# Delta-rule triangular doubling: small products of consecutive issue moved to different partition quarters, one PSUM bank per step

## The chip, the cores and the metric

The kernel runs on one core of a Trainium2 chip. The metric is the device time of one execution in microseconds, as the median over several runs. Lower is better.

## The reference, cut to what matters

The program is two residual blocks with many matrix products. The part at issue is the gated delta rule of the first block: per head it solves a unit lower triangular system for each chunk of the sequence.

```python
kk = jnp.einsum('cbhtd,cbhsd->cbhts', kc, kc)
a_mat = jnp.where(strict, bc[..., :, None] * kk * decay_mat, 0.0)
lhs = a_mat + jnp.eye(CHUNK, dtype=a_mat.dtype)
rhs = jnp.concatenate([vc * bc[..., None], kc * (bc * jnp.exp(gam))[..., None]], axis=-1)
sol = lax.linalg.triangular_solve(lhs, rhs, left_side=True, lower=True, unit_diagonal=True)
```

There are 16 heads of width 128 and 256 positions. Around it stand the large projections: x (256 x 2048) times weights of 2048 x about 20,000 columns in the first block, and more in the second.

## The kernel before, in words

The kernel keeps the large products exact enough by splitting each operand into a high and a low part (`hi`, `lo`) and issuing three matmuls for each weight tile: L156, L157 and L158 in the helper `proj_T` (256 columns, output tile `pT`) and L171, L172 and L173 in the helper `proj` (512 columns, output tile `pN`). ScalarE writes `hi` (L139) and VectorE `lo` (L140). These products fill TensorE through the whole program.

The delta rule is worked in four groups of four heads (`for hg in range(4)`), with the sequence in two halves of 128 positions, so that a group holds eight 128 x 128 triangular matrices, `i = 0..7`. `Ud(i // 4, i % 4)` is the strictly upper part of matrix `i`; `X` becomes the inverse of the unit triangular matrix. It is built by doubling: VectorE inverts the 16 x 16 diagonal blocks (`Xs`), and they come back through DRAM as `Xd` (128 partitions x 8 matrices x 32 columns, the partition quarter `Q[q]` holding the diagonal 32 x 32 block `q`), with the transposed blocks in `Gd`. Then:

- 16 to 32: for each quarter q and matrix i, `wp` = U block times G block (L651), ScalarE copies `-wp` to `W` (L652), `cp` = W times X (L656), and VectorE copies the new 16 x 16 corner to `Xd` (L658). VectorE transposes `Xd` to `Gd` (L659), GpSimd spreads them into `X` and `G` (L661, L663).
- 32 to 64: the same for the pairs of quarters (0, 1) and (2, 3): `wp` (L669), `W` (L670), `cp` (L674), copy to `X` (L675); and the transposed corner `gp_` (L678), copied to `G` (L679).
- 64 to 128: products of 64 x 64 (L683, L688); then the solution is applied with products of 128 x 128 (L695, L699, L703 and on).

Each small product reads its stationary and its moving operand from one quarter of the partitions and writes one quarter: in the first step, quarter q to quarter q; in the second, rows of quarter 0 to quarter 1, and 2 to 3, and back. A small product is one matmul in the program; in fp32 the trace shows two weight loads and two matmul records for it, called two passes here. `side()` hands out one of four buffers of one PSUM bank each (pool `psB`), in turn. In the kernel before, L651 and L656 have two buffers each, used by quarters of even and of odd number, and every quarter of the second step has a buffer of its own; so two quarters that follow one another lie in different banks. Where two runs of the loop share a buffer (`wps[0]` for quarters 0 and 2), the second waits until ScalarE has read the first.

The order on each engine is set by a scheduler when the program is built: it fills the waits of this chain with the projections' matmuls, which are independent of it. TensorE then takes its instructions in that order.

Of the kernel before, what the change touches and what calls it, by code (L numbers as in the profile page):

```python
# [11 lines left out]
AF = mybir.ActivationFunctionType  # L12
# [4 lines left out]
P = 128  # L17
# [67 lines left out]
def hybrid_block_kernel(  # L85
# [4 lines left out]
    act, ve, pe, gp = nc.scalar, nc.vector, nc.tensor, nc.gpsimd  # L90
# [13 lines left out]
    def side(shape=(P, 512), name="s"):  # L104
        return psB.tile(list(shape), F32, tag="s", name=name)
# [94 lines left out]
    with ExitStack() as b1:  # L200
# [139 lines left out]
        with s1:  # L340
# [46 lines left out]
            cps = side([P, 2, 24], name="cps")  # L387
# [131 lines left out]
        with ExitStack() as s2:  # L519
# [37 lines left out]
            XX = X.rearrange("p a b c -> p (a b) c")  # L557
            G = dn.tile([64, 8, 64], F32, name="G")
            gp.memset(X, 0.0)
            gp.memset(G[0:32, :, 32:64], 0.0)  # L560
            zt = dk.tile([P, 256], F32, tag="W", name="zt")
            gp.memset(zt, 0.0)
            nc.sync.dma_start(dram_x.rearrange("m s c -> (m s c)").rearrange("(p c) -> p c", p=P), zt)
            for hg in range(4):
# [46 lines left out]
                Ud = (lambda tt, h: U0[:, h, 0, 0:P] if tt == 0 else U1[:, h, 0, :])  # L611
# [17 lines left out]
                Xd = dn.tile([P, 8, 32], F32, tag="Xd", name="Xd")  # L629
                Gd = dn.tile([P, 8, 32], F32, tag="Gd", name="Gd")  # L630
# [14 lines left out]

                Q = [slice(32 * q, 32 * q + 32) for q in range(4)]
                W = dk.tile([P, 8, 32], F32, tag="W", name="W")
                wps = [side([P, 8, 32], name="wp") for _ in range(2)]
                for q in range(4):
                    for i in range(8):  # L650
                        pe.matmul(wps[q % 2][Q[q], i, :], Ud(i // 4, i % 4)[Q[q], Q[q]], Gd[Q[q], i, :], start=True, stop=True)  # L651
                    act.activation(W[Q[q]], wps[q % 2][Q[q]], AF.Copy, scale=-1.0)  # L652
                cps = [side([P, 8, 32], name="cp") for _ in range(2)]
                for q in range(4):
                    for i in range(8):
                        pe.matmul(cps[q % 2][Q[q], i, :], W[Q[q], i, :], Xd[Q[q], i, :], start=True, stop=True)  # L656
                    r = slice(32 * q, 32 * q + 16)
                    ve.tensor_copy(Xd[r, :, 16:32], cps[q % 2][r, :, 16:32])  # L658
                ve.transpose(Gd, Xd)  # L659
                for q in range(4):  # L660
                    gp.tensor_copy(XX[Q[q], :, Q[q]], Xd[Q[q]])  # L661
# [1 line left out]
                    gp.tensor_copy(G[Q[q], :, Q[q]], Gd[Q[q]])  # L663

                W = dk.tile([P, 8, 32], F32, tag="W", name="W")
                for q in (0, 2):
                    wp = side([P, 8, 32], name="wp")
                    for i in range(8):
                        pe.matmul(wp[Q[q + 1], i, :], Ud(i // 4, i % 4)[Q[q], Q[q + 1]], Gd[Q[q], i, :], start=True, stop=True)  # L669
                    act.activation(W[Q[q + 1]], wp[Q[q + 1]], AF.Copy, scale=-1.0)  # L670
                for q in (0, 2):
                    cp = side([P, 8, 32], name="cp")
                    for i in range(8):
                        pe.matmul(cp[Q[q], i, :], W[Q[q + 1], i, :], Xd[Q[q + 1], i, :], start=True, stop=True)  # L674
                    ve.tensor_copy(XX[Q[q], :, Q[q + 1]], cp[Q[q]])  # L675
                gp_ = side([P, 8, 32], name="gp_")
                for i in range(8):
                    pe.matmul(gp_[Q[1], i, :], Xd[Q[1], i, :], W[Q[1], i, :], start=True, stop=True)  # L678
                ve.tensor_copy(G[Q[1], :, Q[0]], gp_[Q[1]])  # L679

                wp = side([P, 8, 64], name="wp")
                for i in range(8):
                    pe.matmul(wp[64:P, i, :], Ud(i // 4, i % 4)[0:64, 64:P], G[:, i, :], start=True, stop=True)  # L683
                W = dk.tile([P, 8, 64], F32, tag="W", name="W")
                act.activation(W[64:P], wp[64:P], AF.Copy, scale=-1.0)
                cp = side([P, 8, 64], name="cp")
# [6 lines left out]
                wp = side([P, 4, P], name="wp")  # L693
# [3 lines left out]
                cp = side([P, 4, P], name="cp")  # L697
# [3 lines left out]
                wp = side([P, 4, P], name="wp")  # L701
# [162 lines left out]
        with ExitStack() as s4:  # L864
# [66 lines left out]
            for n in range(4):  # L931
# [3 lines left out]
                for kk in range(4):  # L935
                    ps = side([P, T], name="ps")
                    for t in range(2):
# [3 lines left out]
                                   scale=gx[:, 0, k:k + 1], bias=modT[:, 0, k:k + 1])  # L941
# [570 lines left out]
```

## Time and profile before

| | before |
|---|---|
| median of 3 runs (range) | 1936.2 us (1931.1 to 1937.52) |
| profiled execution: time, span | 1928.47 us, 1926.6 us |
| TensorE busy with matmuls | 1892.6 us (98%) |
| VectorE, ScalarE, GpSimd busy | 1491.6, 928.7, 256.7 us |
| granted TensorE clock, mean of the span | 0.995 |

The profiled execution's own time is 7.7 us below the median; what is added to or taken from its span is applied to the median. Busy time of TensorE counts matmuls that overlap one another in a pipeline; what one of them costs is read from the distance between starts.

### The profile page before, as it was taken

Reading aid. Unit: us, or ns where it says so; the run is one execution under the profiler, and the core shown is the slowest. Engines: PE = TensorE matmul, PEld = TensorE weight load, DVE = VectorE, ACT = ScalarE, POOL = GpSimd, SP = SyncE. Lnnn points to the kernel's source line nnn. Section 1 sums busy time; section 2 is a strip of 40 time slices with the busy share of each in tenths; the row PEclk is TensorE's granted clock in tenths of the full one; section 3 lists DMA queues with packets and bytes.
Section 4 is the critical chain, followed back from the end, with each engine's and each line's share of the span. In section 5 each row is a group of like instructions: output and inputs, shape, how many; then the busy total and the mean of one; then the engine's idle time right before and its main releaser. Section 6 shows DMA issues by size and latency. Waiting matters only on the chain. (4 is left out here: it accounts for less than half of the span.)

```text
span 1926.6 us, 31678 instructions
## 1 busy us (share of the span) xinstructions
PE 1892.6 (98%) x12358; PEld 1676.7 (87%) x12358; DVE 1491.6 (77%) x2141; ACT 928.7 (48%) x1240; POOL 256.7 (13%) x371
## 2 busy tenths in 40 slices
PE   9999999999999999999999999999999999999997
PEld 9989898999878898888888887889999998988776
DVE  6978687684648999879995558698787768878976
ACT  7645444453434443444444356663333355555553
POOL 1011010101101221112120000000000023301311
PEclk9999999999999999999999999999999999999999
DMA  8555454454545778768887576663343387557975
GB/s 294 168 165 169 153 169 155 143 176 137 164 158 198 240 258 264 242 222 266 283 284 245 194 258 227 199 212 116 126 148 120 122 288 204 166 174 256 300 248 178
DMA packets 123974, 389.76 MB, mean 202 GB/s; under 512 B 15408, under 2 KB 21976, under 8 KB 123312
## 3 DMA queue, kind: packets, MB, share of 16 engines
q1 hardware_dynamic: 95296, 314.44, 48.7%
q0 software_dynamic: 19296, 54.19, 9.7%
q10 hardware_dynamic: 9232, 19.11, 2.9%
q8 instruction: 97, 1.59, 0.3%
q14 instruction: 53, 0.43, 0.1%
HBM read 368.50 MB, written 16.03 MB: 200 GB/s over the span
## 5 line engine op out<-in xcount | busy, mean ns | idle before, releaser
L139 ACT ACTIVATE hi<-w 128x1024 fp32r<-128x1024 f32 (+1 forms) x535 | 559.1, 1047 | 711.3 <-PE pN L173 393.5
L140 DVE TENSOR_TENSOR lo<-w,hi 128x1024 fp32r<-128x1024 f32 (+1 forms) x535 | 647.7, 1213 | 266.1 <-ACT hi L139 256.7
L172 PE MATMUL pN<-lo,uh 128*128 128x512 f32 x768 | 306.2, 399 | 0.0
L171 PE MATMUL pN<-hi,uh 128*128 128x512 f32 x768 | 304.7, 397 | 0.0
L173 PE MATMUL pN<-hi,ul 128*128 128x512 f32 x768 | 304.5, 396 | 0.0
L156 PE MATMUL pT<-uh,hi 128*128 128x256 f32 x896 | 255.5, 285 | 2.2 <-ACT kq L754 1.9
L158 PE MATMUL pT<-uh,lo 128*128 128x256 f32 x896 | 256.5, 286 | 0.0
L157 PE MATMUL pT<-ul,hi 128*128 128x256 f32 x896 | 255.7, 285 | 0.0
L171 PEld LDWEIGHTS pN<-hi,uh 128*128 128x128 f32 x768 | 145.0, 189 | 33.8
L173 PEld LDWEIGHTS pN<-hi,ul 128*128 128x128 f32 x768 | 145.0, 189 | 33.2
L172 PEld LDWEIGHTS pN<-lo,uh 128*128 128x128 f32 x768 | 145.1, 189 | 33.1
L156 PEld LDWEIGHTS pT<-uh,hi 128*128 128x128 f32 x896 | 168.7, 188 | 5.2 <-ACT kq L754 2.1
L158 PEld LDWEIGHTS pT<-uh,lo 128*128 128x128 f32 x896 | 168.8, 188 | 2.9 <-issue 2.4
L473 DVE SCALAR_TENSOR_TENSOR ma<-m,sc,ma 128x512 f32<-128x512 f32 x240 | 171.1, 749 | 0.0
L157 PEld LDWEIGHTS pT<-ul,hi 128*128 128x128 f32 x896 | 168.8, 188 | 1.8 <-issue 1.2
L463 POOL DMA_DIRECT2D m<-in_w_mod_dram x128 | 69.5, 543 | 287.7 <-DVE ma L473 206.1
L139 ACT ACTIVATE hi<-TT 128x1024 fp32r<-128x1024 f32 x56 | 59.6, 1065 | 77.2 <-PE pK L1064 54.6
L140 DVE TENSOR_TENSOR lo<-TT,hi 128x1024 fp32r<-128x1024 f32 x56 | 68.4, 1223 | 21.0 <-ACT hi L139 20.6
L156 PE MATMUL pT<-hxh,hi 128*128 128x256 f32 x256 | 73.7, 288 | 1.8 <-ACT ra L1165 1.8
L157 PE MATMUL pT<-hxl,hi 128*128 128x256 f32 x256 | 73.0, 285 | 0.0
L158 PE MATMUL pT<-hxh,lo 128*128 128x256 f32 x256 | 73.0, 285 | 0.0
L172 PE MATMUL pN<-lo,hxh 128*128 128x512 f32 x160 | 63.7, 398 | 1.9 <-DVE lo L140 1.8
(729 smaller groups left out, 4053.1 us busy)
## 6 DMA issues: line engine op xcount, KB each, us to landing
w<-in_dn_qkv_dram SPq DMA_DIRECT2D x88, 512.0 KB, 3.2
m<-in_w_mod_dram POOLq DMA_DIRECT2D x128, 256.0 KB, 4.1
w<-in_dn_z_dram SPq DMA_DIRECT2D x32, 512.0 KB, 3.2
w<-in_ml_v_dram SPq DMA_DIRECT2D x32, 512.0 KB, 3.8
w<-in_ml_z_dram SPq DMA_DIRECT2D x32, 512.0 KB, 4.2
w<-in_ml_o_dram SPq DMA_DIRECT2D x32, 512.0 KB, 4.1
w<-in_gate_a_dram SPq DMA_DIRECT2D x32, 512.0 KB, 4.4
w<-in_gate_b_dram SPq DMA_DIRECT2D x32, 512.0 KB, 4.4
```

The source lines that it names most:

```text
L139: act.activation(hi, raw, AF.Copy)
L140: last_lo[0] = ve.tensor_tensor(lo, raw, hi.bitcast(F32), ALU.subtract)
L156: pe.matmul(o, hi[:, k, :], xh[:, kt, :], start=(kt == 0), stop=False)
L157: pe.matmul(o, hi[:, k, :], xl[:, kt, :], start=False, stop=False)
L158: pe.matmul(o, lo[:, k, :], xh[:, kt, :], start=False, stop=(kt == KT - 1))
L171: pe.matmul(ps[:, t, :], xh[:, kt, s], hi[:, k, :], start=(kt == 0), stop=False)
L172: pe.matmul(ps[:, t, :], xh[:, kt, s], lo[:, k, :], start=False, stop=False)
L173: pe.matmul(ps[:, t, :], xl[:, kt, s], hi[:, k, :], start=False, stop=(kt == KT - 1))
L463: (gp if g < 8 else nc.sync).dma_start(raw, d["w_mod"][g, kt])
L473: ve.scalar_tensor_tensor(a, raw, s, a, ALU.mult, ALU.add)
```

## The change

In each step the loops over quarter and matrix are turned: the matrix is now the outer loop and the quarter the inner one, so that consecutive products lie on different quarters. All quarters of a step write one buffer (one bank). In the first step one ScalarE instruction of 128 partitions replaces four of 32 partitions. In the second step the products of `cp` and `gp_` are issued in one loop. The arithmetic of each product stays as it is.

```diff
                 W = dk.tile([P, 8, 32], F32, tag="W", name="W")
-                wps = [side([P, 8, 32], name="wp") for _ in range(2)]
+                wp = side([P, 8, 32], name="wp")
+                for i in range(8):
+                    for q in range(4):
+                        pe.matmul(wp[Q[q], i, :], Ud(i // 4, i % 4)[Q[q], Q[q]], Gd[Q[q], i, :], start=True, stop=True)
+                act.activation(W, wp, AF.Copy, scale=-1.0)
+                cp = side([P, 8, 32], name="cp")
+                for i in range(8):
+                    for q in range(4):
+                        pe.matmul(cp[Q[q], i, :], W[Q[q], i, :], Xd[Q[q], i, :], start=True, stop=True)
                 for q in range(4):
-                    for i in range(8):
-                        pe.matmul(wps[q % 2][Q[q], i, :], Ud(i // 4, i % 4)[Q[q], Q[q]], Gd[Q[q], i, :], start=True, stop=True)
-                    act.activation(W[Q[q]], wps[q % 2][Q[q]], AF.Copy, scale=-1.0)
-                cps = [side([P, 8, 32], name="cp") for _ in range(2)]
-                for q in range(4):
-                    for i in range(8):
-                        pe.matmul(cps[q % 2][Q[q], i, :], W[Q[q], i, :], Xd[Q[q], i, :], start=True, stop=True)
                     r = slice(32 * q, 32 * q + 16)
-                    ve.tensor_copy(Xd[r, :, 16:32], cps[q % 2][r, :, 16:32])
+                    ve.tensor_copy(Xd[r, :, 16:32], cp[r, :, 16:32])
                 ve.transpose(Gd, Xd)
...
                 W = dk.tile([P, 8, 32], F32, tag="W", name="W")
+                wp = side([P, 8, 32], name="wp")
+                for i in range(8):
+                    for q in (0, 2):
+                        pe.matmul(wp[Q[q + 1], i, :], Ud(i // 4, i % 4)[Q[q], Q[q + 1]], Gd[Q[q], i, :], start=True, stop=True)
                 for q in (0, 2):
-                    wp = side([P, 8, 32], name="wp")
-                    for i in range(8):
-                        pe.matmul(wp[Q[q + 1], i, :], Ud(i // 4, i % 4)[Q[q], Q[q + 1]], Gd[Q[q], i, :], start=True, stop=True)
                     act.activation(W[Q[q + 1]], wp[Q[q + 1]], AF.Copy, scale=-1.0)
-                for q in (0, 2):
-                    cp = side([P, 8, 32], name="cp")
-                    for i in range(8):
-                        pe.matmul(cp[Q[q], i, :], W[Q[q + 1], i, :], Xd[Q[q + 1], i, :], start=True, stop=True)
-                    ve.tensor_copy(XX[Q[q], :, Q[q + 1]], cp[Q[q]])
+                cp = side([P, 8, 32], name="cp")
                 gp_ = side([P, 8, 32], name="gp_")
                 for i in range(8):
+                    for q in (0, 2):
+                        pe.matmul(cp[Q[q], i, :], W[Q[q + 1], i, :], Xd[Q[q + 1], i, :], start=True, stop=True)
                     pe.matmul(gp_[Q[1], i, :], Xd[Q[1], i, :], W[Q[1], i, :], start=True, stop=True)
+                for q in (0, 2):
+                    ve.tensor_copy(XX[Q[q], :, Q[q + 1]], cp[Q[q]])
                 ve.tensor_copy(G[Q[1], :, Q[0]], gp_[Q[1]])
```

Line numbers up to L656 are the same in both kernels; behind it the changed kernel's are two to five higher. The scheduler places the chain anew, so the order moves on every engine of this stage. Three places on TensorE follow; a name's number tells buffers apart, and `x8` means eight matmuls of that kind in a row.

TensorE, first head group, the second half of L651 and the first half of L656 in the kernel before (21 matmuls of `pT` stand between the first half of L651 and this):

```order
L157 MATMUL pT_2400<-ul_95,hi_2493 128x256
L651 MATMUL wp_1538<-Gd_1113,U0_1026 32x32 x4
L651 MATMUL wp_1538<-Gd_1113,U1_1027 32x32 x4
L651 MATMUL wp_1539<-Gd_1113,U0_1026 32x32 x4
L651 MATMUL wp_1539<-Gd_1113,U1_1027 32x32 x4
L656 MATMUL cp_1576<-Xd_1112,W_1537 32x32 x8
L656 MATMUL cp_1577<-Xd_1112,W_1537 32x32 x8
L158 MATMUL pT_2400<-uh_94,lo_2494 128x256
```

In the changed kernel, the same head group: all of L651 in one stretch.

```order
L157 MATMUL pT_2393<-ul_95,hi_2456 128x256
L651 MATMUL wp_1538<-Gd_1113,U0_1026 32x32 x16
L651 MATMUL wp_1538<-Gd_1113,U1_1027 32x32 x16
L158 MATMUL pT_2393<-uh_94,lo_2457 128x256
L156 MATMUL pT_2393<-uh_94,hi_2456 128x256
```

Three stretches (half of L651; the other half with half of L656; the rest of L656) have become two, L651 and, 24 matmuls of `pT` behind it, L656 with 32 matmuls into one `cp`.

TensorE, first head group, second step, the kernel before: `cp` of quarter 0, `cp` of quarter 2, then `gp_`.

```order
L158 MATMUL pT_2400<-uh_94,lo_2614 128x256
L674 MATMUL cp_1642<-Xd_1112,W_1621 32x32 x8
L674 MATMUL cp_1652<-Xd_1112,W_1621 32x32 x8
L678 MATMUL gp__1662<-W_1621,Xd_1112 32x32 x8
L156 MATMUL pT_2400<-uh_94,hi_2613 128x256
```

The changed kernel at this place (the pair of rows in the middle comes eight times in all):

```order
L157 MATMUL pT_2393<-ul_95,hi_2576 128x256
L677 MATMUL cp_1636<-Xd_1112,W_1616 32x32 x2
L678 MATMUL gp__1637<-W_1616,Xd_1112 32x32
L677 MATMUL cp_1636<-Xd_1112,W_1616 32x32 x2
L678 MATMUL gp__1637<-W_1616,Xd_1112 32x32
```

The two quarters of `cp` and the one of `gp_` now alternate; the number of products is the same, 24.

TensorE, last head group, the steps to 64 and 128, the kernel before:

```order
L173 MATMUL pN_6327<-hi_6468,ul_95 128x512
L674 MATMUL cp_5494<-Xd_4964,W_5473 32x32 x8
L674 MATMUL cp_5504<-Xd_4964,W_5473 32x32 x8
L678 MATMUL gp__5514<-W_5473,Xd_4964 32x32 x8
L683 MATMUL wp_5524<-G_950,U0_4878 64x64 x4
L683 MATMUL wp_5524<-G_950,U1_4879 64x64 x4
L688 MATMUL cp_5535<-X_949,W_5533 64x64 x8
L171 MATMUL pN_6497<-hi_6500,uh_94 128x512
```

The changed kernel, last head group:

```order
L173 MATMUL pN_6299<-hi_6440,ul_95 128x512
L690 MATMUL cp_5507<-X_949,W_5505 64x64 x8
L697 MATMUL wp_5517<-vv_4309,X_949 128x128 x4
L701 MATMUL cp_5523<-ww_4310,U0_4857 128x128 x4
L171 MATMUL pN_6469<-hi_6472,uh_94 128x512
```

Before, three dependent links of the chain (L678, L683, L688) stand without a projection between them; in the changed kernel these have 24 and 23 matmuls of `pN` between them, and the three links L690, L697, L701 (L688, L695, L699 before) stand together instead.

## Rows read from the trace of the kernel before

**Rows 1.** The page: busy us (share of the span), instructions, of TensorE.
```profile
PE 1892.6 (98%) x12358; PEld 1676.7 (87%) x12358; DVE 1491.6 (77%) x2141; ACT 928.7 (48%) x1240; POOL 256.7 (13%) x371
```

**Rows 2.** Waits of TensorE, 150 to 600 us: who for whom, total, times, longest.
```profile
PE pT L156 <- ACT kq L754: 1.9, 1, 1.9
PE wp L683 <- DVE G L679: 0.7, 1, 0.7
PE cp L688 <- ACT W L685: 0.7, 1, 0.7
```

**Rows 3.** Timeline of TensorE, first group, first half of L651: start, us, instructions.
```profile
168.06 0.28 PE L156 MATMUL pT<-uh,hi 128*128 128x256 f32 x1
168.18 0.28 PE L157 MATMUL pT<-ul,hi 128*128 128x256 f32 x1
168.38 1.09 PE L651 MATMUL wp<-Gd,U 32*32 32x32 f32 x32
169.41 0.38 PE L158 MATMUL pT<-uh,lo 128*128 128x256 f32 x1
169.63 0.28 PE L156 MATMUL pT<-uh,hi 128*128 128x256 f32 x1
```

**Rows 4.** Timeline of TensorE, first group: second half of L651 with half of L656.
```profile
171.88 0.28 PE L157 MATMUL pT<-ul,hi 128*128 128x256 f32 x1
172.08 1.00 PE L651 MATMUL wp<-Gd,U 32*32 32x32 f32 x29
...
173.92 0.38 PE L158 MATMUL pT<-uh,lo 128*128 128x256 f32 x1
174.14 0.28 PE L156 MATMUL pT<-uh,hi 128*128 128x256 f32 x1
```

**Rows 5.** Timeline of TensorE, first group: L674 with L678.
```profile
187.84 0.28 PE L158 MATMUL pT<-uh,lo 128*128 128x256 f32 x1
188.05 1.00 PE L674 MATMUL cp<-Xd,W 32*32 32x32 f32 x29
...
189.48 0.38 PE L156 MATMUL pT<-uh,hi 128*128 128x256 f32 x1
189.70 0.28 PE L157 MATMUL pT<-ul,hi 128*128 128x256 f32 x1
```

**Rows 6.** Timeline of TensorE, second group, 299.2 to 299.45 us.
```profile
299.04 0.41 PE L651 MATMUL wp<-Gd,U 32*32 32x32 f32 x8
299.26 0.21 PE L656 MATMUL cp<-Xd,W 32*32 32x32 f32 x1
299.28 0.21 PE L651 MATMUL wp<-Gd,U 32*32 32x32 f32 x2
299.32 0.19 PE L656 MATMUL cp<-Xd,W 32*32 32x32 f32 x1
299.32 0.20 PE L651 MATMUL wp<-Gd,U 32*32 32x32 f32 x2
299.35 0.19 PE L656 MATMUL cp<-Xd,W 32*32 32x32 f32 x1
```

**Rows 7.** Instructions on the tile `wp`: count, ns min/median/max, first and last start.
```profile
L651 PE MATMUL wp<-Gd,U x256: 191/191/212, 168.4 to 543.4; 32*32 32x32 f32 x128
L669 PE MATMUL wp<-Gd,U x128: 191/191/212, 184.2 to 557.4; 32*32 32x32 f32 x128
L652 ACT ACTIVATE W<-wp x16: 357/375/378, 169.1 to 543.6; 32x256 f32<-32x256 f32 x16
```

**Rows 8.** Timeline of TensorE, last group, with its idle time in brackets.
```profile
560.78 1.11 PE L683 MATMUL wp<-G,U 64*64 64x64 f32 x16 [0.68 <-DVE G L679]
562.58 1.97 PE L688 MATMUL cp<-X,W 64*64 64x64 f32 x16 [0.68 <-ACT W L685]
```

**Rows 9.** Windows, last group: stretch, its length, PE busy, granted clock, DMA share, GB/s.
```profile
555.00:561.80 6.80, 6.12 (x107) 1.00 0.49 164
561.80:568.70 6.90, 6.22 (x28) 0.51 0.51 152
568.70:575.00 6.30, 6.30 (x32) 1.00 0.26 86
```

## The prediction

> **What bounds the kernel now.** I read the page first, then the waits of TensorE in the stage of the delta rule, then its timeline around the small products. TensorE has a matmul in flight for 98% of the span and the next engine is at 77% [rows 1]. In the 450 us around the four head groups it hardly waits: the three longest waits come to 3.3 us [rows 2]. So an instruction taken off TensorE's stream shortens the program by what it took there, and time saved on another engine is worth nothing as long as TensorE does not wait for it. The matter is what the small products cost in the stream.
>
> That cost is read from starts, since matmuls overlap. The `pT` matmuls around the products start 0.12 us apart [rows 3]. The first half of L651 (16 products, 32 passes) stands between the starts at 168.18 and 169.63, 1.45 us; without it there would be two steps of 0.12 there. It costs 1.21 us. Its own passes start over 1.09 - 0.19 = 0.90 us, and the other 0.32 us is a fixed price of going from the large products to the small ones and back. The second half of L651 with half of L656 (64 passes) costs 174.14 - 171.88 - 0.24 = 2.02 us [rows 4], and L674 with L678 (48 passes) 189.70 - 187.84 - 0.24 = 1.62 us [rows 5]. The rest of L656 and L669 are stretches of 32 passes like the first, 1.21 us each (L669 has half the passes of L651, with the same 191 ns for one [rows 7]). A head group costs 1.21 + 2.02 + 1.21 + 1.21 + 1.62 = 7.27 us in five stretches with 208 passes; four groups 29 us. That is all the change can touch directly, 1.5% of the span.
>
> **What sets the pace of a pass.** Within one quarter eight passes start over 0.41 - 0.19 = 0.22 us, 31.4 ns apart [rows 6]. Then comes the one place in the trace where three quarters meet: four passes of L656 on quarter 0 stand between L651 on quarter 2 and on quarter 3. From 299.26 six passes start within 0.09 us, 15 ns apart or less, while L656 alone goes on at about 32 ns (299.32, 299.35) [rows 6]. So 31.4 ns is the step of one quarter, and streams on different quarters run beside one another. In the kernel before they meet only at the borders of the loops, because eight products on one quarter (16 passes) follow one another. Turned loops make every neighbour a border.
>
> **The change part by part, per head group.**
> - L651 and L656, 64 passes each: with four quarters at once, 16 steps, so the starts span 15 x 31.4 = 0.47 us and a little stagger, 0.49. With 0.32 fixed: 0.81 us each. From the other side, had only the pace of 15 ns been kept, 63 x 15 = 0.95, so 1.27 each.
> - L669, 32 passes on two quarters: 0.47 + 0.32 = 0.79 us.
> - L677 with L678, 48 passes: `cp` reads quarters 1 and 3, `gp_` reads quarter 1 again. No row shows two products that read the same quarter and write different ones. If each takes its turn, quarter 1 has 32 passes, 31 x 31.4 = 0.97, and with 0.32 it is 1.29 us; if they run side by side, 0.79. I take 1.29, since the only row of one quarter is that of strict turns.
> - Sum: 0.81 + 0.81 + 0.79 + 1.29 = 3.70 us in four stretches, against 7.27 in five. The gain is 3.57 us per group, of which 0.32 is the stretch that fell away, and 14.3 us for four. At the pace of 15 ns it is 2 x 0.46 less per group, 10.6 us; with `gp_` side by side 2.0 more, 16.3 us.
> - ScalarE: four copies of about 0.375 us per group [rows 7] become one. That it frees is worth nothing on the path. What could cost is that L656 now waits for one copy behind all of L651. The order puts 24 `pT` matmuls there in the first group, 24 x 0.12 = 2.9 us; the copy, even taken as twice 0.375, fits with over 2 us to spare for whatever ScalarE is in. VectorE's four copies per group keep their number and come one after another; they have 43 `pT` matmuls before L669 is due, over 5 us. I cost both at nothing. Without that cover each would cost its own length, under 2 us per group.
> - Waits for a buffer: the second half of L651 waited for ScalarE to empty `wps[0]`. That wait was covered before (no row of it among the longest [rows 2]), so it gives nothing by itself; its going is what lets the stretches merge.
> - The last group: L678, L683 and L688 stood together and TensorE idled 0.68 us twice [rows 8], and then its granted clock was at 0.51, the 1.2 GHz level, for 6.9 us [rows 9]; that took at most half of 6.9, 3.4 us. In the new order these three are covered and L690, L697, L701 stand together instead, with two waits of the same kind (a copy by VectorE, a copy by ScalarE). I take the idle time as the same, 1.4 us, and the fall of the clock as repeated; if it is not, up to 3.4 us more are gained.
>
> The profiled execution would go from 1928.5 to 1914.2 us. The median stands 7.7 us above it, and the same gain on it gives 1936.2 - 14.3 = **1921.9 us**.
>
> **The rivals.**
> 1. *One bank takes one quarter at a time, with a stall.* Every overlap that the trace shows is between buffers, so between banks: 299.26 has `cp`, `wp` of quarter 2 and `wp` of quarter 3 in three [rows 6]. The change puts all quarters of a step in one. If a product must wait until the one before it has left the bank, the price of a pass rises above its 31.4 ns. The point of no gain is (7.27 - 4 x 0.32) / 208 = 29 ns a pass; above 36 ns (7 ns more, 832 passes, 5.8 us) the kernel is slower by more than 0.3%. If a pass waits out the whole 191 ns of its record [rows 7], a group costs 208 x 0.191 + 1.3 = 41 us and the program 136 us more, 2072 us. Against it: the quarters write different partitions of that bank, and nothing in the rows says that a pass holds more than its own. The Trainium skill has a rule that speaks for it (TensorEngine Tiling (Array Packing), Restrictions and Gotchas): different row tiles write to different banks and cannot access the same bank at the same time. No run so far shows it either way.
> 2. *One bank serialises, without more.* Then a pass costs 31.4 ns whatever its neighbour: 2 x (63 x 0.0314 + 0.32) + 1.29 + 1.29 (`gp_` has its own bank) = 7.2 us per group. The turn gives nothing, and the time stays within 1 us of 1936.
> 3. *There is a floor under the distance of starts.* If instructions came to the array no faster than one pass in about 27 ns on average, as over all of rows 4 (64 passes from 172.08 to about 173.8), then 208 x 0.027 + 1.3 = 6.9 us, and the gain is 1.5 us in all: 1934.7. Against it: six starts in 0.09 us [rows 6]. Those may have been instructions that had queued up, so it is not excluded. The Trainium skill names such a floor (TensorE: Matmul & The Clock Gate, "Wait — 56ns, not 53.3ns?"), about 25 ns from start to start however small the product. The trace disagrees where quarters differ, with its 15 ns.
> 4. *The new order opens waits.* The schedule differs from here up to the end of the first block. TensorE waited once for 1.9 us [rows 2]; several such, with the clock falling behind one, would take 5 to 10 of the 14 us: about 1929 us.
>
> **How the numbers follow.** Four quarters in parallel in one bank (gain 10.6 to 16.3, with the clock up to 19.7): 0.72. Rival 2: 0.08. Rival 3: 0.07. Rival 4: 0.05. Rival 1: 0.08. 0.3% of 1936 us is 5.8 us, about what a measurement of this kernel can tell from no change. Faster than 1930.4: the first case and half of the fourth, 0.75. Within 0.3%: rivals 2 and 3 and the rest of 4, 0.17. Slower: 0.08. For the range, 1936.2 - 19.7 = 1916.5 and 1936.2 - 10.6 = 1925.6 bound the first case; the runs shown lie up to 5 us from their median, of which I add 3 below and 3 above, and 4 more above for new waits: 1913 to 1933 us. That holds the first case and rival 4, and leaves out 1, 2 and most of 3.
>
> **What would show it.** Right: the stretch of L651 with 64 passes spans about 0.5 us from its first start to its last, and starts come some 8 ns apart; L669 about 0.5; L677 with L678 about 1.0; four stretches per group. The four groups end some 14 us earlier against the start of the program, and behind them the distance stays. Wrong: passes 31 ns apart or more in L651 although the quarter changes (rivals 1 and 2; near 191 ns it is the first), 25 to 27 ns (rival 3), or idle time on TensorE behind L656 or L690 that is not there before (rival 4). The prediction falls if one bank cannot take four quarters at once; all else moves it by a few microseconds.

## The result, and the profile after

| | before | changed |
|---|---|---|
| median (range, runs) | 1934.16 us (1931.1 to 1937.52, 4) | 1913.43 us (1910.05 to 1916.28, 4) |
| profiled execution: time, span | 1928.47, 1926.6 us | 1912.48, 1910.3 us |

The ratio is 0.9894, with a 95% interval of 0.9879 to 0.9909: 17.6 to 23.4 us less, by the medians 20.7. The medians of before in the sections below are those of its runs on the same chip as the experiment.

The page of the changed kernel, TensorE's part of the busy times (answers to [rows 1]):

```profile
PE 1876.2 (98%) x12358; PEld 1661.7 (87%) x12358; DVE 1492.5 (78%) x2141; ACT 924.2 (48%) x1228; POOL 265.6 (14%) x371
```

As many matmuls, 16.4 us less of them in flight; the other engines do what they did, ScalarE with twelve instructions fewer. The timeline of TensorE at the four stretches of the first head group (start, us, instructions; answers to [rows 3], [rows 4] and [rows 5]):

```profile
168.18 0.28 PE L157 MATMUL pT<-ul,hi 128*128 128x256 f32 x1
168.38 0.75 PE L651 MATMUL wp<-Gd,U 32*32 32x32 f32 x64
169.07 0.39 PE L158 MATMUL pT<-uh,lo 128*128 128x256 f32 x1
169.29 0.28 PE L156 MATMUL pT<-uh,hi 128*128 128x256 f32 x1
...
172.11 0.75 PE L656 MATMUL cp<-Xd,W 32*32 32x32 f32 x64
...
178.09 0.69 PE L670 MATMUL wp<-Gd,U 32*32 32x32 f32 x32
...
182.14 0.28 PE L157 MATMUL pT<-ul,hi 128*128 128x256 f32 x1
182.35 0.22 PE L677 MATMUL cp<-Xd,W 32*32 32x32 f32 x2
182.37 0.21 PE L678 MATMUL gp__1637<-W,Xd 32*32 32x32 f32 x1
...
182.86 0.19 PE L678 MATMUL gp__1637<-W,Xd 32*32 32x32 f32 x1
182.98 0.38 PE L158 MATMUL pT<-uh,lo 128*128 128x256 f32 x1
183.21 0.28 PE L156 MATMUL pT<-uh,hi 128*128 128x256 f32 x1
```

(L670 is the L669 of before, L677 its L674; `gp_` is on L678 in both.) L651 starts at the same 168.38 us in both programs. All its 64 passes start within 0.75 - 0.19 = 0.56 us, where half of them took 0.90 before. The stretch costs 169.29 - 168.18 - 0.24 = 0.87 us. L656 is the same; L670 spans 0.69 - 0.19 = 0.50 us; L677 with L678 spans 0.51 and costs 183.21 - 182.14 - 0.24 = 0.83. A group costs 0.87 + 0.87 + 0.82 + 0.83 = 3.39 us, against 7.27 before. The other three groups give the same spans, but for L677 with L678 in the second, where the products stand in another order and span 0.59.

The waits of TensorE from 150 to 600 us (who for whom, total, times, longest), and the two places in the last group with the idle time in brackets (answers to [rows 2] and [rows 8]):

```profile
PE wp L697 <- DVE X L691: 0.8, 1, 0.8
PE cp L701 <- ACT ww L698: 0.7, 1, 0.7
```

```profile
542.89 1.14 PE L690 MATMUL cp<-X,W 64*64 64x64 f32 x16
544.81 1.16 PE L697 MATMUL wp<-vv,X 128*128 128x128 f32 x8 [0.78 <-DVE X L691]
546.66 1.16 PE L701 MATMUL cp<-ww,U 128*128 128x128 f32 x8 [0.69 <-ACT ww L698]
```

The idle time moved from L683 and L688 to L697 and L701 and is as long. The 1.9 us behind L754 is gone. The windows there (stretch, length, busy times, granted clock; answers to [rows 9]) show no fall of the clock:

```profile
541.00:549.00 8.00, 6.54 (x47) 5.35 (x46) 4.86 (x5) 2.94 (x4) 0.00 (x0) 1.00 0.41 140
549.00:555.00 6.00, 6.00 (x37) 5.18 (x36) 1.23 (x1) 1.66 (x3) 0.00 (x0) 1.00 0.15 51
```

Behind this stage the distance stays for a while. The 5600th matmul from the end of the program is the same instruction in both. Before:

```profile
1002.79 0.40 PE L172 MATMUL pN<-lo,uh 128*128 128x512 f32 x1
```

and in the changed kernel:

```profile
982.12 0.40 PE L172 MATMUL pN<-lo,uh 128*128 128x512 f32 x1
```

That is 20.7 us gained by there. From the matmul at 168.18, the last one ahead of the first L651, to this one it is 834.6 us before and 813.9 in the changed kernel; the sections below call this the stage distance, and the same two matmuls bound it in every version. The two profiled spans differ by 16.3 only: in the second block, where TensorE's order is unchanged, this execution of the changed kernel gave 4 us back; why is not followed here. That the medians differ by 20.7 too is in part chance, with an interval from 17.6 to 23.4.

### The profile page after: what moved, and what is told of

The parts are those of the page before. It is cut to its first block, busy times and chain, and to the rows that moved or that the text cites. A ratio compares the mean times of both kernels' runs of the same rounds, so it can differ in the third digit from the quotient of the medians.

```text
span 1910.3 us, 31664 instructions
## 1 busy us (share of the span) xinstructions
PE 1876.2 (98%) x12358; PEld 1661.7 (87%) x12358; DVE 1492.5 (78%) x2141; ACT 924.2 (48%) x1228; POOL 265.6 (14%) x371
```

## The experiments

All numbers of TensorE below are read like those above. Edits are against the changed kernel.

**e1_turned_banks_apart.** Turned loops, but the buffers of before.

```diff
-                wp = side([P, 8, 32], name="wp")
+                wps = [side([P, 8, 32], name="wp") for _ in range(2)]
...
-                        pe.matmul(wp[Q[q], i, :], Ud(i // 4, i % 4)[Q[q], Q[q]], Gd[Q[q], i, :], start=True, stop=True)
-                act.activation(W, wp, AF.Copy, scale=-1.0)
-                cp = side([P, 8, 32], name="cp")
+                        pe.matmul(wps[q % 2][Q[q], i, :], Ud(i // 4, i % 4)[Q[q], Q[q]], Gd[Q[q], i, :], start=True, stop=True)
+                for q in range(4):
+                    act.activation(W[Q[q]], wps[q % 2][Q[q]], AF.Copy, scale=-1.0)
+                cps = [side([P, 8, 32], name="cp") for _ in range(2)]
```

(and likewise two buffers of `wp` and of `cp` in the second step)

> The loops are turned as in the change, but the buffers stay as they were before: two banks for each product of the first step (quarters of even and odd number apart), one bank for each quarter of the second step. Theory (the pace is that of one tile, a read quarter with a write quarter; tiles run side by side whatever their bank): 64 passes of L651 span 0.56 us as in the changed kernel, 32 passes of the second step 0.50, 48 passes 0.51, and the time is that of the changed kernel plus about 2 us for other stretches, 1913 to 1917 us. Rival (the bank counts): the spans differ from those of the changed kernel by more than 0.05 us and the time by more than 5 us.

Measured: 1918.22 us, ratio to before 0.9930 (0.9912 to 0.9948). The timeline of its L651:

```profile
168.19 0.28 PE L157 MATMUL pT<-ul,hi 128*128 128x256 f32 x1
168.40 0.75 PE L651 MATMUL wp<-Gd,U 32*32 32x32 f32 x64
169.09 0.39 PE L158 MATMUL pT<-uh,lo 128*128 128x256 f32 x1
```

0.75 us with two banks, 0.75 with one: quarters of one bank are written side by side as freely as those of two. The time missed the theory's range: it is some 5 us above the changed kernel by the medians, 7 by the ratios, and the stage distance is 4.3 us longer. The spans are those of the changed kernel, so the bank is not the cause. The scheduler's other order put waits of 1.9 us (two in all) and 1.7 us into this stage, where the changed kernel has 0.8 and 0.7:

```profile
PE hp L739 <- DVE gz L734: 1.9, 2, 1.7
PE cp L691 <- ACT W L688: 1.7, 1, 1.7
```

and in two groups it broke L656 (here L657) into pieces, three stretches more in all. In this execution the granted clock also fell once in the stage, to the level of 1.2 GHz, which took at most half of 3.4 us:

```profile
466.20:469.60 3.40, 3.40 (x23) 3.34 (x23) 2.53 (x8) 0.00 (x0) 1.16 (x1) 0.50 0.11 20
```

**e2_one_bank_old_loops.** One bank and one copy as in the change, but the quarter outside again. The stretches and the projections between them stand in the same order as in the changed kernel, but for one stretch of the last group that comes one matmul of `pN` earlier.

```diff
-                for i in range(8):
-                    for q in range(4):
+                for q in range(4):
+                    for i in range(8):
                         pe.matmul(wp[Q[q], i, :], Ud(i // 4, i % 4)[Q[q], Q[q]], Gd[Q[q], i, :], start=True, stop=True)
```

(and so for `cp`, and for the three products of the second step)

> One bank per product, one copy by ScalarE and the same stretches as in the changed kernel, but the quarter is the outer loop again, as before. Theory: 64 passes span 63 x 31.4 ns less some 0.09 us at each of three borders of quarters, 1.7 us; 32 passes 0.90 and 48 passes 1.31 us. Each head group costs 2 x 1.15 + 0.40 + 0.80 = 3.5 us more than in the changed kernel, 14 us in all: 1927 us. Rival (the gain came from fewer stretches, one copy, the new order and the clock, not from the turn): 1913 to 1918 us. Second rival (products of one bank do not overlap at a border): 64 passes span 1.98 us, and the time is 1930 us.

Measured: 1928.68 us, ratio to before 0.9975 (0.9964 to 0.9986). Its L651:

```profile
167.51 0.28 PE L157 MATMUL pT<-ul,hi 128*128 128x256 f32 x1
167.72 1.91 PE L651 MATMUL wp<-Gd,U 32*32 32x32 f32 x64
169.56 0.38 PE L158 MATMUL pT<-uh,lo 128*128 128x256 f32 x1
...
995.41 0.40 PE L172 MATMUL pN<-lo,uh 128*128 128x512 f32 x1
```

The passes span 1.91 - 0.19 = 1.72 us: the theory's 1.7, not the 1.98 without overlap at the borders. It is 15 us slower than the changed kernel, with the same two waits (0.8 and 0.7 us) and nearly the same order, so the turn alone is worth that. The stage distance says the same of one execution: 995.41 - 167.51 = 827.9 us, 14.0 more than the changed kernel's 813.9. The rival, that fewer stretches, the one copy and the new order brought the gain, is left with what e2 gains on before: 0.25%, about 5 us, and 6.7 of the stage distance.

**e3_first_step_only.** The second step is that of before (the lower half of the change's diff undone).

> Only the first step (16 to 32) is turned and put in one bank; the second step is that of before. Theory: the second step costs 0.90 and 1.31 us of passes instead of 0.50 and 0.51, 1.2 us per group, 4.8 us in all: 1918 us. Rival (the parts do not add, the order decides): off by more than 3 us from that, with waits on TensorE that the changed kernel does not have.

Measured: 1917.27 us, ratio 0.9921 (0.9906 to 0.9936), against the theory's 1918. The spans are 0.56, 0.56, 0.90 and 1.31 us. It has one wait, of 1.6 us at L700 (the changed kernel's L701), where the changed kernel has 0.8 and 0.7: as much in all. The parts add within 1 us: the stage distance is 4.5 us above the changed kernel's, against the theory's 4.8.

**e4_second_step_only.** The first step is that of before (the upper half undone).

> Only the second step (32 to 64) is turned and put in one bank; the first step is that of before. Theory: 1.2 us per group gained against the kernel before, 4.8 us in all, to which comes what the order makes of the wait of 1.9 us and of the slow clock in the last group (2.7 us): 1925 to 1930 us. Rival (the second step opens waits that eat its gain): 1932 to 1936 us.

Measured: 1929.38 us, ratio 0.9987 (0.9975 to 0.9999): inside the 1925 to 1930 expected, but by ratio only 2.5 us, and 2.4 of the stage distance, are gained of the 4.8 that its passes save (0.50 and 0.51 us in each group). Its waits of TensorE, 150 to 600 us, the longest:

```profile
PE pT L156 <- ACT kq L755: 1.9, 1, 1.9
PE bp L597 <- DVE D L599: 1.9, 2, 1.6
```

The first is the wait of before [rows 2], the second is new. So a part of the rival is right: an order that the scheduler makes anew can hold back 2 us of 5.

**e6_eight_tiles.** Is there a floor? A tile is a read quarter with a written one. Every product of L651 is issued twice, the second time into the next quarter of a spare bank that nobody reads.

```diff
                         pe.matmul(wp[Q[q], i, :], Ud(i // 4, i % 4)[Q[q], Q[q]], Gd[Q[q], i, :], start=True, stop=True)
+                        pe.matmul(sp_[Q[(q + 1) % 4], i, :], Ud(i // 4, i % 4)[Q[q], Q[q]], Gd[Q[q], i, :], start=True, stop=True)
```

> Adds work: each product of L651 is issued a second time into the next quarter of a spare bank that nobody reads, so that 128 passes on eight tiles follow one another in a stretch. Theory without a floor (each tile steps at 31.4 ns, whatever runs beside it): the 128 passes span about 0.6 us, hardly more than the 64 of the changed kernel with their 0.56. Rival (the distance of starts has a floor near the 8.9 ns of the changed kernel): 127 x 8.9 ns = 1.13 us.

Measured (one execution): 1918.54 us. From the timeline of TensorE, the first rows, some from the middle, and the last:

```profile
168.03 0.21 PE L652 MATMUL wp<-Gd,U 32*32 32x32 f32 x1
168.04 0.21 PE L653 MATMUL sp__1539<-Gd,U 32*32 32x32 f32 x1
...
168.19 0.19 PE L653 MATMUL sp__1539<-Gd,U 32*32 32x32 f32 x1
168.27 0.22 PE L652 MATMUL wp<-Gd,U 32*32 32x32 f32 x2
...
168.36 0.21 PE L652 MATMUL wp<-Gd,U 32*32 32x32 f32 x2
168.38 0.21 PE L653 MATMUL sp__1539<-Gd,U 32*32 32x32 f32 x2
168.39 0.21 PE L652 MATMUL wp<-Gd,U 32*32 32x32 f32 x2
168.41 0.21 PE L653 MATMUL sp__1539<-Gd,U 32*32 32x32 f32 x2
...
169.12 0.19 PE L653 MATMUL sp__1539<-Gd,U 32*32 32x32 f32 x1
```

128 passes start over 169.12 - 168.03 = 1.09 us, 8.6 ns apart, and in the middle two come every 17 ns. Over the stretch twice the tiles bring no faster pace than four: the rival's 1.13 us is right, the theory's 0.6 is not. But 8.6 ns is an average, and not the least distance of two starts. The first 32 passes start from 168.03 to 168.19, 5 ns apart; then none starts for 0.08 us, and only from there do two come every 17 ns. So eight tiles did run faster than four as long as the first 32 passes lasted. That these had queued up, and that the later ones come no faster than they are delivered, would look like this; no run shows it. The 64 passes of the changed kernel are 0.56 / 63 = 8.9 ns apart, near the later pace.

**e7_pairs.** Two quarters at a time in the first step.

```diff
-                for i in range(8):
-                    for q in range(4):
+                for i, q in [(i, p + j) for p in (0, 2) for i in range(8) for j in range(2)]:
```

(and so for `cp` of the first step)

> First step with two quarters at a time: the products alternate between quarters 0 and 1 for all eight matrices, then between 2 and 3. Theory: each half steps at 31.4 / 2 ns, the two halves overlap a little at their border: 64 passes span about 1.0 us against 0.56 with four quarters and 1.72 with one; the program is some 0.45 x 8 = 3.5 us longer than the changed kernel, about 1917 us. Rival (alternation alone is what counts, two quarters are enough): 0.56 to 0.6 us.

Measured (one execution): 1912.08 us. Its L650, the products of L651:

```profile
168.83 0.28 PE L157 MATMUL pT<-ul,hi 128*128 128x256 f32 x1
169.04 1.11 PE L650 MATMUL wp<-Gd,U 32*32 32x32 f32 x64
...
985.59 0.40 PE L172 MATMUL pN<-lo,uh 128*128 128x512 f32 x1
```

The passes span 1.11 - 0.19 = 0.92 us, between one quarter's 1.72 and four quarters' 0.56: the theory, a little quicker, and not the rival's 0.6. Eight such stretches lose 8 x 0.36 = 2.9 us. The time of one execution can't show that, but the trace can: TensorE's order is that of the changed kernel, and the stage distance is 985.59 - 168.83 = 816.8 us, 2.8 more than there.

**e8_halves_of_64.** Can the 64 x 64 products be quickened in the same way?

```diff
-                    pe.matmul(wp[64:P, i, :], Ud(i // 4, i % 4)[0:64, 64:P], G[:, i, :], start=True, stop=True)
+                    for q in (2, 3):
+                        pe.matmul(wp[Q[q], i, :], Ud(i // 4, i % 4)[0:64, Q[q]], G[:, i, :], start=True, stop=True)
```

(and `cp` of the next step into quarters 0 and 1)

> The changed kernel, and the 64 x 64 products (two steps of 8 products, 16 passes over 0.92 us each) are split by output columns into halves of 32 that alternate between two quarters of the output: twice the products, half the weight columns each. Theory (a step is weights and moving columns of one tile in turn, 64 + 64 columns in 61.5 ns now; 32 + 64 columns would take about 46 ns on two tiles side by side): 32 passes span 15 x 46 ns = 0.7 us, 0.2 us less, 8 stretches: 1.7 us less than the changed kernel, 1912 us, too little for the timing and to be read from the trace. Rival (products that read the same rows of the array take turns): 31 x 46 ns = 1.4 us, 4 us slower than the changed kernel.

Measured: 1918.44 us, ratio 0.9920 (0.9906 to 0.9933). Its stretch, and the same one of the changed kernel behind it, each from its own timeline:

```profile
189.61 1.08 PE L686 MATMUL wp<-G,U 64*32 64x64 f32 x32
```

```profile
189.43 1.14 PE L685 MATMUL wp<-G,U 64*64 64x64 f32 x16
```

The starts span 0.87 us against 0.92 (1.08 and 1.14 less the 0.22 of one record, from unrounded times): 0.05 us less, neither the 0.2 gained of the theory nor the loss of the rival. The starts in the trace are 0, 7, 80, 87, 136, 143, 192 and 199 ns from the first, and so on: the two halves of a product start 7 ns apart, side by side as the theory has it, and do not take turns. The step from one pair to the next was mis-sized: 80 ns once and then 56, where the theory had 46. What sets it is open. The kernel is slower than the changed one, by 2.0 us of the stage distance, although each stretch is shorter: its order has waits of 1.9 us (L754's again) and 1.8 us in this stage, 2.2 more than the changed kernel's two. No version run here beats the changed kernel beyond the scatter of the runs.

## Why the prediction was right, point by point

The median came to 1913.43 us, 8.5 below the forecast 1921.9 and 0.4 above the lower end of the range. Of the 8.5, 2.0 belong to the kernel before (1936.2 us over three runs, 1934.16 with a fourth), and 6.4 to a gain of 20.7 in place of 14.3. That is the best case of the forecast, 19.7, and a little more; only the 3 us that it allowed for scatter kept the time inside.

- **TensorE's stream is the bound, and a pass costs its distance of starts.** Right. e2 and the changed kernel differ in the loop order alone, and 15 us of time, 14.0 of the stage distance, answer to 14.0 us of passes: 2 x (1.72 - 0.56) + (0.90 - 0.50) + (1.31 - 0.51) = 3.5 us a group.
- **31.4 ns is the step of one quarter, and quarters run beside one another.** Right: one quarter at a time 1.72 us, two 0.92, four 0.56 for 64 passes. The overlap does not reach far: a border of the old order saves only (1.98 - 1.72) / 3 = 0.09 us (e2), some three steps, so the neighbour on another quarter has to come almost at once.
- **Four quarters in one bank.** Right; this was the forecast's condition. e1 shows that banks apart give the same 0.56 us, and e2 that even the borders of the old order overlap in one bank. Rivals 1 and 2 fall. The Trainium skill (TensorEngine Tiling (Array Packing), Restrictions and Gotchas) says that different row tiles cannot access one bank at the same time. The trace shows no price of it: on four quarters 64 passes span 0.56 us in one bank as in two (e1). These products also differ in the quarter that they write. In e6 two tiles write the same quarter, of different banks, and the first 32 passes start 5 ns apart all the same; the same quarter of one bank was not tried.
- **The floor (rival 3).** A limit exists, but at an average of 8.6 ns a pass over a long stretch (e6), not at the 27 I worked with; so four quarters just fit. It cost the first step 0.07 us a stretch against my 0.49, 0.6 us in all. The rival's doubt about the six starts at 299.26, that they may have been instructions that had queued up, has something to it: the first 32 passes of e6 came faster than the rest. The Trainium skill (TensorE: Matmul & The Clock Gate, "Wait — 56ns, not 53.3ns?") has about 25 ns from start to start as the least. The traces agree on one tile, with 31.4 ns, and not across tiles, with 8.6.
- **L677 with L678.** The term was mis-sized: I let the two products that read quarter 1 take turns, 1.29 us; they run side by side, 0.83, as my other bound had it. That is 1.8 us more in all. A stream is a pair of quarters, one read and one written.
- **One stretch fewer per group** at 0.32 us: right by the starts around the stretches (0.87 - 0.56 = 0.31).
- **The last group, and new waits (rival 4).** I took the idle time, the wait of 1.9 us and the fall of the clock as staying. The idle time stayed. The wait went, 1.9 us, and the clock did not fall, at most 3.4. That L656 waits for one copy by ScalarE cost nothing, as forecast: TensorE's two waits of the changed kernel are elsewhere.

By sizes: 14.3 forecast, + 1.8 for L678, - 0.6 for the pace, + 1.9 for the wait, come to 17.4. Two short waits of before are gone too, which I had not counted:

```profile
PE p L604 <- DVE hbl L188: 0.3, 1, 0.3
PE pT L156 <- DVE gz L639: 0.2, 1, 0.2
```

With them it is 17.9. Up to the matmul at 982 us the trace has 20.7, so 2.8 remain. The clock's 6.9 us at half speed fit that. Before, the passes of L688 span 1.97 - 0.37 = 1.60 us there [rows 8], against 0.92 elsewhere, and eight matmuls of `pN` behind them start 0.43 us apart, against 0.23; two of them:

```profile
566.77 0.63 PE L173 MATMUL pN<-hi,ul 128*128 128x512 f32 x1
567.20 0.63 PE L171 MATMUL pN<-hi,uh 128*128 128x512 f32 x1
```

That is 0.7 + 8 x 0.2 = 2.3 us by these rows alone, and at most 3.4. So the mechanism was right and the gain forecast too small by a third, for two reasons: one term read from its cautious bound, and a schedule that I held to stay where it was.

What stays open is the clock. In the profile of e6 the last group has the order and the two waits of the changed kernel (0.78 and 0.69 us), and there the clock fell (windows: stretch, length, busy times, granted clock):

```profile
541.00:549.00 8.00, 6.54 (x43) 5.15 (x42) 3.97 (x4) 3.74 (x4) 0.00 (x0) 1.00 0.45 140
549.00:552.40 3.40, 3.40 (x13) 3.01 (x14) 0.89 (x2) 0.00 (x0) 0.00 (x0) 0.50 0.41 154
```

So a single fall is not settled by the order. Over many runs the clock goes with it all the same. On one chip the mean granted clock of the span is 0.9941 over 23 runs of before and 0.9942 over 12 of e4, which keeps the last group's order of before; it is 0.9959 over 12 runs of e2 and 0.9963 over 6 of e3, which have the changed kernel's order or nearly so. A difference of 0.0018 over 1930 us is at most 3.5 us. It is not the turn by itself: e1 is turned, with an order of its own, and has 0.9943. What in the order does it, no run separates. Nor is it controlled what the order itself is worth: 0.25% in e2, and in e1, e4 and e8 orders that hold back 2 to 5 us.

## What to carry to other kernels

Small products on TensorE, such as the 32 x 32 in fp32 here, are cheapest when consecutive ones use different pairs of read and written quarters: one pair steps at 31.4 ns, and other pairs fill that step until starts come some 8.5 ns apart on average, here with four. Read the price of an instruction in a pipelined stream from the distance of starts, and look in the trace for a place where the new neighbourhood happens by chance, as at 299.26 us; before the change was run it told that quarters overlap, though its 15 ns was only an upper bound of the pace. To compare two versions by one trace each, take the distance between two matmuls that both have, ahead of the change and behind it. Where a scheduler orders the program, allow a few microseconds either way for the waits that a new order opens or closes.

## What was not expected of the hardware

The pace of 8.6 ns for a weight load with its matmul over 128 passes, although the first 32 start 5 ns apart (e6), and that two tiles which read the same 32 partitions do not slow each other: 48 passes on three tiles span 0.51 us with quarter 1 read by two of them, as 32 passes on two tiles span 0.50. And splitting 64 x 64 products into halves by output columns gains only 0.05 us of 0.92, although the halves start 7 ns apart (e8).
